# A norm row loaded once and spread over the partitions by products with ones, and the first chunk prepared ahead of the sample

## The chip, the core and the metric

The kernel runs on one core of a Trainium2 chip. A core has TensorE (matrix products, and turning of tiles by a product with the identity), VectorE, ScalarE and GpSimd (elementwise work), and SyncE, which mostly issues transfers. Transfers are issued from SP's and ACT's queues and run on 16 shared DMA engines. The metric is the time of one execution in microseconds, as the median of several runs.

## What is computed

One step of a decoder trunk of two layers: a retention layer with 4 heads, then a sliding-window attention layer. The prompt has 1024 tokens and the sample 8 tokens, all of 1024 features in f32. What matters here is the head of the first layer:

```python
def rmsnorm(x, g):
    xf = x.astype(jnp.float32)
    y = xf * lax.rsqrt(jnp.mean(xf * xf, axis=-1, keepdims=True) + EPS)
    return (y * g.astype(jnp.float32)).astype(x.dtype)

def retention_layer(x, S0, g_norm, w_in, g_out, w_out):
    h = rmsnorm(x, g_norm)
    proj = h @ w_in        # 1024 x 6144: q, k, v and gate
    ...
```

The norm's gain g_norm is one row of 1024 values (4 KB). Every token, prompt or sample, is multiplied by it.

## The kernel before

The whole kernel is one program with the order of each engine's instructions written out by hand. The prompt is cut into eight chunks of 128 tokens, X[0] to X[7], with tokens on the partitions and 1024 features along the row; X[8] holds the 8 sample tokens. Each chunk goes through the same steps, each a small helper:

- xload (L426): the transfer of the chunk, on SP's queue.
- sq (L431): ScalarE squares the chunk and sums each row.
- pw (L435 and L120): GpSimd turns the sum into one over the root, in two small instructions.
- sc (L440): VectorE multiplies the chunk by that column and by gb, the norm row spread over all 128 partitions.
- TR (through tr, L105): TensorE turns the chunk in eight 128 by 128 products into two banks of PSUM.
- hi and lo (L457, L461): ScalarE rounds the turned chunk to the short form, and VectorE takes the remainder; keep (L465) copies it back.

The first weights, a set called q0 with four tiles A11, A12, A21 and A22, are split in the same way by w_hi (ScalarE, L221) and w_lo (GpSimd or VectorE, L226). The first products are 16 "plain" groups of 24 products each (L544); chunks 1 and 3 to 7 are prepared between these groups, in an order given slot by slot. After them come the products of the projection by a seven-product scheme, the retention stage, and the second layer.

The program's start is written out in order: memsets, the load of gb as a broadcast of the 4 KB row to 128 partitions on ACT's queue (L866), the identity on the same queue (L867), the loads of chunk 0, the sample, chunk 2, two q0 tiles, chunks 1 and 3, two tiles of the next set, and chunks 4, 6 and 7 on SP's queue. Then the squares and roots of the sample, of chunk 0 and of chunk 2; the sample is scaled and turned first (eight small products into p8), then chunk 0 is scaled and turned. VectorE copies p8 to rdec and scales chunk 2, TensorE turns chunk 2, and hi, lo, w_hi and w_lo of chunks 0 and 2 and of A11 and A12 follow. Engines take their instructions in the written order, so an instruction that waits holds up those behind it on its engine.

The buffers called raw, five in turn, hold weight tiles and chunk 7. Chunks 4, 5 and 6 and the sample share three buffers called u; chunk 5 takes the sample's.

Of the kernel before, what the change touches and what calls it, by code (L numbers as in the profile page):

```python
# [7 lines left out]
F32 = mybir.dt.float32  # L8
# [6 lines left out]
D = 1024  # L15
# [45 lines left out]
def trunk(tc, x_prompt, x_sample, state_ret, cache_k, cache_v, norm_ret, w_in_ret, ret_out_norm,  # L61
          w_out_ret, norm_swa, w_in_swa, q_norm, k_norm, sinks, w_out_swa, c1, c2,
          y_p, y_s, nrp, nrs, nkp, nvp, nks, nvs):
    nc = tc.nc
    ctx = ExitStack()
    with ctx:
        ctx.enter_context(tc.manual_schedule(engines=MS))
        _trunk(ctx, tc, nc, locals())


def _trunk(ctx, tc, nc, a):
    x_prompt, x_sample, state_ret = a["x_prompt"], a["x_sample"], a["state_ret"]
    cache_k, cache_v = a["cache_k"], a["cache_v"]
    norm_ret, ret_out_norm, norm_swa = a["norm_ret"], a["ret_out_norm"], a["norm_swa"]
# [22 lines left out]
    mm = nc.tensor.matmul  # L97
# [6 lines left out]
    def tr(out, in_, ident, start=True, stop=True):  # L104
        nc.tensor.matmul(out, in_, ident, is_transpose=True, start=start, stop=stop)  # L105
# [13 lines left out]
    def rsq(out, in_, n):  # L119
        nc.gpsimd.tensor_tensor(out, in_, mhalf[:in_.shape[0], :n], ALU.pow)  # L120
# [13 lines left out]
    dcp = sa.enter_context(tc.tile_pool(name="dcp", bufs=1, reuse_waits="tile"))  # L134
    wq = sa.enter_context(tc.tile_pool(name="wq", bufs=1, reuse_waits="tile"))
# [26 lines left out]
    def bank(i, t):  # L162
        return abp.tile([128, 512], F32, tag=f"b{i}{t}", name=f"b{i}{t}")
# [7 lines left out]
    act, dve, pool = nc.scalar.activation, nc.vector, nc.gpsimd  # L171
# [238 lines left out]
    gb = sp.tile([128, D], F32, name="gb")  # L410
# [6 lines left out]
    def xload(c):  # L417
        if c in (0, 1, 2, 3):
            X[c] = xq.tile([128, D], F32, tag="xq", bufs=4, name="xq")
        elif c == 7:  # L420
            X[c] = raw_tile()
        else:
            X[c] = sp.tile([128, D], F32, tag="u", bufs=3, name="u")
        if c == 8:
            X[c] = X[c][0:ND, :]
        nc.sync.dma_start(out=X[c], in_=x_sample[:, 0, :] if c == 8 else x_prompt[0, c * 128:c * 128 + 128, :])  # L426

    def sq(c):
        SS[c] = sp.tile([128, 1], F32, name="ss", bufs=4)
        n = X[c].shape[0]  # L430
        act(junk[:n], X[c], AF.Square, accum_out=SS[c][:n])  # L431

    def pw(c):
        n = X[c].shape[0]
        pool.tensor_scalar(SS[c][:n], SS[c][:n], 1.0 / D, EPS, MUL, ADD)  # L435
        rsq(SS[c][:n], SS[c][:n], 1)

    def sc(c):
        n = X[c].shape[0]
        dve.scalar_tensor_tensor(X[c], X[c], SS[c][:n], gb[:n], MUL, MUL)  # L440

    def TR(c, b):

        PO[c] = [bank(b, j).rearrange("p (k t) -> p k t", k=4) for j in range(2)]
        for j in range(2):
            for k in range(4):
                tr(PO[c][j][:, k, :], X[c][:, 512 * j + k * 128:512 * j + k * 128 + 128], ident)
# [415 lines left out]
    for r in range(2):  # L863
        pool.memset(oneh[:, r, r:r + 1], 1.0)
    pool.memset(rdec32, 0.0)
    nc.scalar.dma_start(out=gb, in_=norm_ret[0].partition_broadcast(128))  # L866
    nc.scalar.dma_start(out=ident, in_=a["c1"][:, 0:128])  # L867
    act(warm, warm, AF.Silu)
    for c in (0, 8, 2):
        xload(c)  # L870
# [5 lines left out]
        raw_load(k0, r, nc.sync)  # L876
    for c in (4, 6, 7):
        xload(c)
    for c in (8, 0, 2):
        sq(c)  # L880
        pw(c)
    sc(8)
    p8 = vdp.tile([128, 8, ND], F32, tag="vd", name="pd8")
    for k in range(8):
        tr(p8[:, k, :], X[8][:, k * 128:k * 128 + 128], ident[:ND, :ND])
    sc(0)
    TR(0, 1)
    dve.tensor_copy(rdec, p8)
    sc(2)
    TR(2, 2)  # L890
# [1357 lines left out]
    out = so_all()  # L2248
# [159 lines left out]
```

## Time and profile before

| What | Value |
|---|---|
| median of 3 runs | 1294.03 us (1293.03 to 1294.62) |
| time of the profiled execution | 1293.47 us |
| its span, first to last instruction | 1291.7 us |
| TensorE busy | 1268.1 us, 98% |
| VectorE, GpSimd, ScalarE busy | 766.3, 741.4, 668.2 us |
| moved by the DMA engines | 206.69 MB |

The profile is of one execution; the time around the span, 1293.47 less 1291.7, belongs to the start and end of the program. Starts in the views are counted from the first instruction of the span.

### The profile page before, as it was taken

To read this page: it belongs to the slowest core of one execution; us is meant where nothing else is said; L and a number is where in the kernel's file an instruction comes from. 1 tells how busy PE (TensorE), PEld (TensorE's weight loads), DVE (VectorE), ACT (ScalarE), POOL (GpSimd) and SP (SyncE) were. 2 spreads that over 40 slices of the span, in tenths; PEclk is the share of its full clock that TensorE was granted. 3 is DMA by queue.
4 is the path that set the end of the run, shared out by engine and by line. 5 is a ranking of instruction groups with operands and counts; after the bars stand their busy time and mean duration, and the time that the engine had idled before them with its cause. 6 is when DMAs were issued, how large, how long until landed. Compare 5 with 4: busy or idle time off the path is not lost.

```text
span 1291.7 us, 26846 instructions
## 1 busy us (share of the span) xinstructions
PE 1268.1 (98%) x9839; PEld 1216.2 (94%) x9839; DVE 766.3 (59%) x1474; ACT 668.2 (52%) x1656; POOL 741.4 (57%) x886
## 2 busy tenths in 40 slices
PE   6999999999999999999999999999999999999998
PEld 5999999999999999988889999999999999998998
DVE  5954646665576764476763656855566666765321
ACT  5533445454555554588761234545575766765121
POOL 5654444535359899798771458636585767544000
PEclk9999999999999999999999999999998999999999
DMA  6313857677667673556879855833031221137232
GB/s 227 108 54 121 253 183 237 179 253 218 186 210 226 192 239 107 180 173 218 255 211 261 229 195 153 272 113 103 15 118 50 66 66 58 54 119 249 78 92 79
DMA packets 221967, 206.69 MB, mean 160 GB/s; under 512 B 32728, under 2 KB 196820, under 8 KB 221820
## 3 DMA queue, kind: packets, MB, share of 16 engines
q1 hardware_dynamic: 189840, 170.61, 43.8%
q10 hardware_dynamic: 31996, 34.36, 8.2%
q8 instruction: 78, 1.28, 0.4%
q14 instruction: 53, 0.43, 0.1%
HBM read 135.41 MB, written 70.55 MB: 159 GB/s over the span
## 4 chain that ended last, share of the span: by engine, by line
PE 90%; DVE 3%; DMA 2%; POOL 1%; ACT 1%; issue 1%; SPq 0%; ACTq 0%; DVEq 0%; POOLq 0%
PE b L335 8%; PE b L336 8%; PE b L337 8%; PE S L1302 7%; PE pj L1661 6%; PE pj L1662 6%; PE pj L1663 6%; PE b L328 4%; PE tr L105 4%; PE b L329 4%; PE b L330 4%; PE o L2023 2%; PE b L544 1%; PE sc L1986 1%; PE S L335 1%; PE S L336 1%
## 5 line engine op out<-in xcount | busy, mean ns | idle before, releaser
L335 PE MATMUL b<-xh,woh 128*128 128x258 f32 x784 | 223.2, 285 | 0.0
L337 PE MATMUL b<-xh,wol 128*128 128x258 f32 x784 | 221.7, 283 | 0.0
L336 PE MATMUL b<-xl,woh 128*128 128x258 f32 x784 | 221.6, 283 | 0.0
L1661 PE MATMUL pj<-SA,wh 128*128 128x384 f32 (+1 forms) x496 | 169.3, 341 | 1.5 <-ACT SA L2043 1.3
L1662 PE MATMUL pj<-SA,wh 128*128 128x384 f32 (+1 forms) x496 | 159.4, 321 | 0.2 <-DVE SA L2044 0.2
L1663 PE MATMUL pj<-SA,wl 128*128 128x384 f32 (+1 forms) x496 | 159.4, 321 | 0.0
L335 PEld LDWEIGHTS b<-xh,woh 128*128 128x128 f32 x784 | 148.0, 189 | 4.1 <-issue 3.7
L336 PEld LDWEIGHTS b<-xl,woh 128*128 128x128 f32 x784 | 148.7, 190 | 0.0
L337 PEld LDWEIGHTS b<-xh,wol 128*128 128x128 f32 x784 | 148.0, 189 | 0.0
L226 POOL TENSOR_TENSOR wol<-raw,woh 128x512 fp32r<-128x512 f32 x51 | 66.2, 1306 | 120.3 <-ACT woh L221 109.2
L328 PE MATMUL b<-woh,xh 128*128 128x256 f32 x448 | 126.6, 283 | 0.0
L329 PE MATMUL b<-wol,xh 128*128 128x256 f32 x448 | 126.0, 281 | 0.0
L330 PE MATMUL b<-woh,xl 128*128 128x256 f32 x448 | 125.6, 280 | 0.0
L1661 PEld LDWEIGHTS pj<-SA,wh 128*128 128x128 f32 x496 | 94.1, 190 | 5.1 <-issue 2.4
L1662 PEld LDWEIGHTS pj<-SA,wh 128*128 128x128 f32 x496 | 94.3, 190 | 0.4 <-DVE SA L2044 0.4
L2001 POOL TENSOR_TENSOR s<-s,sm 128x512 f32<-128x512 f32 x64 | 66.6, 1041 | 48.2 <-DVE sm L2000 43.2
L1663 PEld LDWEIGHTS pj<-SA,wl 128*128 128x128 f32 x496 | 93.9, 189 | 0.0
L328 PEld LDWEIGHTS b<-woh,xh 128*128 128x128 f32 x448 | 84.3, 188 | 5.0 <-issue 2.9
L330 PEld LDWEIGHTS b<-woh,xl 128*128 128x128 f32 x448 | 84.3, 188 | 0.0
L329 PEld LDWEIGHTS b<-wol,xh 128*128 128x128 f32 x448 | 84.3, 188 | 0.0
L1993 ACT ACTIVATE s<-s,mx 128x257 f32<-128x257 f32 x128 | 64.2, 505 | 34.9 <-DVE mx L1991 34.2
L221 ACT ACTIVATE woh<-s 128x512 fp32r<-128x512 f32 x88 | 54.1, 624 | 54.4 <-POOL s L211 20.7
(530 smaller groups left out, 3622.6 us busy)
## 6 DMA issues: line engine op xcount, KB each, us to landing
raw<-in_w_in_ret_dram ACTq DMA_DIRECT2D x44, 512.0 KB
st<-in_state_ret_dram SPq DMA_DIRECT2D x64, 256.0 KB
out_dram<-st SPq DMA_DIRECT2D x64, 256.0 KB
vb<-vscr SPq DMA_DIRECT2D x64, 128.0 KB
evp<-qks SPq DMA_DIRECT2D x32, 256.0 KB
evx<-vsc SPq DMA_DIRECT2D x32, 256.0 KB
wr<-in_w_in_swa_dram SPq DMA_DIRECT2D x32, 256.0 KB
evc<-gsc SPq DMA_DIRECT2D x16, 256.0 KB
```

Of the source, the lines that this page charges most:

```text
L226: eng.tensor_tensor(lo, src_of(s, name, sub), hi.bitcast(F32), SUB)
L328: mm(dst, xh, wh, start=a and i == 0, stop=False, skip_group_check=True)
L329: mm(dst, xh, wl, start=False, stop=False, skip_group_check=True)
L330: mm(dst, xl, wh, start=False, stop=z, skip_group_check=True)
L335: mm(dst, wh, xh, start=a, stop=False, **sg)
L336: mm(dst, wh, xl, start=False, stop=False, **sg)
L337: mm(dst, wl, xh, start=False, stop=z, **sg)
L1302: mm(box[0], s.op[f"A{i + 1}{j + 1}", 0][w][:, k, :], xs_[t][x[j]][:, k, :], start=(xs_ is XH and w == 0 and j + k == 0), stop=(xs_ is XL ...
L1661: mm(ps, hi[:, k, fs], xh[:, k, t0:t1], start=first and k == ks[0], stop=False)
L1662: mm(ps, hi[:, k, fs], xl[:, k, t0:t1], start=False, stop=False)
L1663: mm(ps, lo[:, k, fs], xh[:, k, t0:t1], start=False, stop=last and k == ks[-1])
L2001: nc.gpsimd.tensor_tensor(st[:, :, 0:256], st[:, :, 0:256], sm.unsqueeze(2).broadcast_to([128, 2, 256]), ALU.mult)
```

## The change

The norm row is loaded as it is, 4 KB, into the first partition of a raw buffer. A row of 128 ones (row1) is made by VectorE. Two products of the ones with the halves of the row put the row on all partitions of two PSUM banks, and VectorE copies these to gb. The order of the first three chunks becomes chunk 0, sample, chunk 2 for the squares and roots; chunk 0 is scaled and turned ahead of the sample's scaling and turning.

```diff
-    nc.scalar.dma_start(out=gb, in_=norm_ret[0].partition_broadcast(128))
+    grow = wq.tile([1, D], F32, tag="raw", bufs=5, name="raw")
+    nc.scalar.dma_start(out=grow, in_=norm_ret[0:1, :])
     nc.scalar.dma_start(out=ident, in_=a["c1"][:, 0:128])
+    row1 = dcp.tile([1, 128], F32, name="row1")
+    dve.memset(row1, 1.0)
     act(warm, warm, AF.Silu)
...
-    for c in (8, 0, 2):
+    bank_of = {}
+    for j in range(2):
+        bank_of[0, j] = bank(0, j)
+        mm(bank_of[0, j], row1, grow[:, 512 * j:512 * j + 512], start=True, stop=True)
+    for j in range(2):
+        dve.tensor_copy(gb[:, 512 * j:512 * j + 512], bank_of[0, j])
+    for c in (0, 8, 2):
         sq(c)
         pw(c)
+    sc(0)
+    TR(0, 1)
     sc(8)
     p8 = vdp.tile([128, 8, ND], F32, tag="vd", name="pd8")
     for k in range(8):
         tr(p8[:, k, :], X[8][:, k * 128:k * 128 + 128], ident[:ND, :ND])
-    sc(0)
-    TR(0, 1)
     dve.tensor_copy(rdec, p8)
     sc(2)
     TR(2, 2)
```

## Rows read from the trace of the kernel before

**Rows 1.** The page, busy time of TensorE, its share of the span, instructions.

```profile
PE 1268.1 (98%) x9839; PEld 1216.2 (94%) x9839; DVE 766.3 (59%) x1474; ACT 668.2 (52%) x1656; POOL 741.4 (57%) x886
```

**Rows 2.** Stretches: length, TensorE's busy time and instructions, granted clock, DMA share, GB/s.

```profile
24.00:53.20 29.20, 28.78 (x242) 1.00 0.23 71
53.20:500.00 446.80, 446.80 (x3762) 1.00 0.64 194
```

**Rows 3.** Chain of waits of the start: start, length, what.

```profile
1.17 5.33 DMA u<-in_x_sample_dram
...
8.94 1.01 POOL ss L435
...
10.02 0.58 POOL ss L120
...
11.97 1.97 PE b L105 x8
...
16.91 3.81 POOL wol L226 x3
...
50.83 1.21 DVE raw L440
```

**Rows 4.** Queues (packets, MB) to 2.5, 3.0, 6.5 us; 6.5 to 7.0; SP's wait.

```profile
q1 hardware_dynamic: 21, 0.09, 21.4%
...
q10 hardware_dynamic: 16, 0.07, 5.3%
...
q1 hardware_dynamic: 215, 0.78, 39.2%
q10 hardware_dynamic: 288, 0.59, 29.6%
...
6.50:7.00 0.50, 0.00 (x0) 0.00 (x0) 0.00 (x0) 0.48 (x1) 0.00 (x0) 1.00 1.00 410
...
SPq L426 <- DMA gb<-in_norm_ret_dram: 2.5, 1, 2.5
```

**Rows 5.** Timeline to 38 us: start, length, engine, line, what, idle time before.

```profile
0.72 0.41 ACTq L866 DMA_DIRECT2D gb<-in_norm_ret_dram  x1
...
7.70 1.06 ACT L431 ACTIVATE junk<-xq 128x1024 f32<-128x1024 f32 x1
...
9.94 1.02 PE L105 MATMUL pd<-ident,u 8*128 8x8 f32 x8 [9.94 <-DVE u L440]
...
11.83 0.22 DVE L888 COPY rdec<-pd 128x64 f32<-128x64 f32 x1
...
12.64 1.28 DVE L440 SCALAR_TENSOR_TENSOR xq<-xq,ss,gb 128x1024 f32<-128x1024 f32 x1 [0.59 <-POOL ss L120]
...
15.78 0.74 PE L544 MATMUL b<-xh,woh 128*128 128x258 f32 x4
...
19.82 1.12 PE L544 MATMUL b<-xh,woh 128*128 128x258 f32 x8
...
21.65 2.30 DVE L440 SCALAR_TENSOR_TENSOR xq<-xq,ss,gb 128x1024 f32<-128x1024 f32 x1 [3.41 <-POOL ss L120]
...
21.75 1.13 PE L544 MATMUL b<-xl,woh 128*128 128x258 f32 x8
...
24.10 1.06 PE L105 MATMUL b<-ident,xq 128*128 128x128 f32 x8 [1.23 <-DVE xq L440]
...
36.78 1.15 ACT L481 ACTIVATE xh<-xq 128x512 fp32r<-128x512 f32 x2 [1.53 <-DMA gl<-in_norm_swa_dram]
```

**Rows 6.** Lines: an f32 product of 512 columns; copies of a PSUM bank; ns min/median/max.

```profile
L344 PE MATMUL vd<-raw,rdec x64: 592/592/617, 76.8 to 331.6; 128*32 128x512 f32 x64
...
L465 DVE COPY xq<-b x4: 673/678/679, 17.0 to 25.1; 128x512 f32<-128x512 f32 x4
```

**Rows 7.** Line L105, turning products before 15.2 us and after 24, ns min/median/max.

```profile
L105 PE MATMUL b<-ident,xq x14: 364/421/477, 12.0 to 15.1; 128*128 128x128 f32 x14
...
L105 PE MATMUL b<-ident,xq x16: 271/273/302, 24.1 to 28.7; 128*128 128x128 f32 x16
```

## The prediction

> **What bounds the kernel now.** I read the page first: TensorE is busy for 98% of the span [rows 1]. So only two things can move the time: less TensorE work, or TensorE starting sooner. The change does not remove TensorE work, so I went to the stretches [rows 2]. From 53.2 to 500 us TensorE is busy for all of 446.8 us; from 24 to 53.2 it lacks 0.4 us; before 24 lie its waits. The change sits wholly at the start, before the plain products at 15.78 [rows 5]. A gain there is worth what it takes off the moment when TensorE begins its unbroken work, and no more; after it everything is issued relative to what came before, so the shift should be carried to the end.
>
> Next the chain of waits for the start [rows 3]. It begins with the load of the sample's chunk (landed at 6.50), then ScalarE's sums of squares, GpSimd's root for chunk 0 (its first half takes 1.01 us), VectorE's scaling of chunk 0, TensorE's turning of chunks 0 and 2, and the conversion of the second weight tile, after which GpSimd starts three weight remainders at 16.91. From there the chain runs through GpSimd and VectorE to the scaling of chunk 7 at 50.83, and joins TensorE there. TensorE and this second chain arrive together: TensorE waited 1.23 us for chunk 1 at 24.10 and then all but 0.4 us of the way was work. Hence the quantity to forecast is the shift of GpSimd's start at 16.91.
>
> **The transfers.** The broadcast row is 512 KB and goes on ACT's queue beside chunk 0 (512 KB) on SP's. Up to 6.5 us the two queues had moved 0.59 and 0.78 MB [rows 4]: the row took about half of what moved. It falls to 4 KB. When does chunk 0 land then? Up to 2.5 us SP's queue had moved 0.09 MB, all chunk 0 at that time. Left are 0.524 - 0.09 = 0.43 MB and 0.066 MB of the identity; at the 410 GB/s of [rows 4] that is 1.2 us: 3.7 us is the lower bound. The same sum for the kernel before (1.15 MB up to the sample, less 0.09) gives 5.1, and the sample landed at 6.5, 1.4 later; so 5.1 is the upper bound. I take 4.3, nearer the lower, since less than half the bytes can lag. SP also waited 2.5 us at chunk 3's load for the broadcast to land [rows 4]; that goes, but ScalarE squares chunk 3 only behind the first plain group [rows 5], so it is worth nothing.
>
> The 4 KB row itself: a 4 KB load later in the kernel kept ScalarE waiting 1.53 us [rows 5], so it took at least about that; the sample's load took 5.33 [rows 3]. Issued at 0.72 as the broadcast was [rows 5], it lands between 2.2 and 6.1. ACT's queue moves its first packets between 2.5 and 3.0 [rows 4], and this row is the first on it: I take 3.2.
>
> **The products and copies.** No row shows a product with one partition. The nearest is the f32 product of 512 columns, 592 ns [rows 6], taken late at the faster rate. Early on the same turning products take 421 ns against 273 later [rows 7], and eight of them 1.97 us [rows 3] against 1.06 [rows 5]. The granted-clock column reads 1.00 throughout [rows 2]; the durations say otherwise, and I read the early ones as the 1.2 GHz level. So a product costs between 0.59 and 1.18 us; I take 1.18, since TensorE has done nothing before. Two products end at 3.3 + 2.4 = 5.7, and the second copy out of the bank (0.68 [rows 6]) makes the row ready at 6.4; the first copy hides under the second product. Copies and products lie where TensorE was idle until 9.94 and VectorE until it scaled the sample just before that [rows 5]. The memset of the ones, the extra buffer turn (chunk 7 now takes the row's buffer, and its load is the last of those on SP) and SP's own order cost nothing for the same reason. Bounds for the ready time: 2.2 + 1.2 + 0.7 + 0.2 = 4.3, and 6.1 + 2.4 + 0.7 + 0.1 = 9.3.
>
> **The new order.** Chunk 0 at 4.3: squares 1.06 and the reading of the sum, 1.15 together (squares 7.70 to 8.76 [rows 5], the sum read just behind); GpSimd's two small steps with nothing beside them about 0.95 more (their first half has 1.01 in the chain because of company, their second 0.58 [rows 3]; I take the first at under 0.4). So its scaling can start at 6.4, just when the row is ready. That first half took 1.01 before because VectorE's scaling of the sample ran beside it; now it is free, and the sample's own step pays instead.
>
> From the scaling's start S, step by step: 1.28 + 0.06, turning of chunk 0 1.97, then the sample's eight small turns 1.02 (its scaling, from about S + 1.9 to S + 3.2, is done by then), then the copy of them on VectorE 0.22 with gaps, together S + 4.65, and only then chunk 2's scaling, which stands behind that copy on VectorE. Before, chunk 2's scaling waited for GpSimd's root alone (12.64 [rows 5]); that root now ends near S + 3.8. So the reordering puts a new wait in front of chunk 2: 0.65 us is given back there, since sample landing to chunk 2 was 12.64 - 6.50 = 6.1 and is now 2.1 + 4.65 = 6.75.
>
> With S = 6.4, chunk 2 is scaled at 11.05 instead of 12.64: 1.6 us sooner, and with it its turning, the weight conversion and GpSimd's 16.91. ScalarE reaches chunk 2's squares at about 6.7, after the load. The sample moves later by a little; its columns and the reload of its buffer (chunk 5, squared among the plain groups) have slack.
>
> **Sum.** Span 1291.7 - 1.6 = 1290.1; 1.8 us lie outside the span (1293.47 - 1291.7), so 1291.9; the profiled execution stood 0.56 under the median of 1294.03. Forecast 1292.4. Bounds: S = 5.8 (early chunk, fast products) gives -2.2; chunk 0 at 5.1 gives S = 7.2 and -0.8; a row ready only at 9.3 gives +1.3.
>
> **The clock.** Before, the turns run without a gap from 11.97, and the first plain products at 15.78 run at the fast rate (four in 0.74 us, the pace of the later blocks of eight in 1.12 [rows 5]). After, TensorE's work comes as islands: products until 5.7, turns 7.8 to 10.8, a gap of 1.6, turns from 12.4. The faster level may come later. A group of 24 plain products takes 2.9 us at the fast rate (three blocks, 19.82 to 21.75 and 1.0 more [rows 5]), so it would lose up to 2.9 at half of it. Up to 24.10 TensorE has 1.2 us of waiting to absorb this. The Trainium skill (TensorE: Matmul & The Clock Gate, Part 4) says that transposes don't count as busy for the clock; by it the islands would change nothing, the plain products would start slow in both kernels, the sum would stay and the third rival would have no chance. The trace disagrees: the plain products at 15.78 ran at the fast pace with only turns before them [rows 5].
>
> **Rivals.** (1) *The row or chunk 0 comes late.* If the row lands after 4.75, S + 4.65 passes 12.64 and the start is later than before; at the bound it is +1.3, so 1295.3. If chunk 0 doesn't land sooner at all (6.4), the change does not do what it is for: S = 8.5, +0.5, 1294.5. For it: nothing shows a lone 4 KB row in a loaded start. Against: it is first on its queue, and half the bytes ahead of chunk 0 are gone. With gains under 0.8: 0.18. (2) *More is gained.* Chunk 1's scaling took 2.30 us instead of 1.28 beside a weight remainder on GpSimd [rows 5]; if it slips past that one, another 1.0 comes off exactly where TensorE waits: -2.6, 1291.4; with S at its low bound -3.2, 1290.8. Chance 0.17. (3) *The clock, and slower.* If the 1.2 GHz level holds past the second plain group, two groups cost 5.8, less the 1.2 of waiting and the 1.6 gained: +3.0, 1297.0. It decides from the end of the first group: one alone costs 2.9 against those 2.8, no change. Against: turns alone raised the rate before. Chance 0.05.
>
> **How the numbers follow.** The forecast with its own range of 1291.6 to 1293.2 gets 0.58, and 0.02 stays for what I don't see. About 0.2%, 2.6 us, is what can be told from no change here; the three runs spread over 1.6. Faster by more than that needs 1291.4 or less: rival 2 and the forecast's lower tail, 0.18. Slower by that: rival 3 and little else, 0.05. The rest, 0.77, is within. The range of 1290.6 to 1294.4 leaves out the far ends of rivals 2 and 1 and all of 3.
>
> **What would show it.** Chunk 0 is squared first, at 4.3 (3.7 to 5.1); the row's two copies end by 6.4; chunk 0's scaling waits for one of the two; the sample's GpSimd step is now the long one; chunk 2's scaling starts straight after the small copy, near 11.05; GpSimd's three remainders start near 15.3 instead of 16.91; chunk 1's turning starts near 22.5; TensorE's work from 53.2 on keeps its length. It would be wrong if the three remainders start early and the end of chunk 7's turning doesn't follow, or if the clock's level after 12 us differs.

## The result, and the profile after

The changed kernel took 1296.79 us (median of 11, 1293.93 to 1299.29) beside 1293.32 for the kernel before on the same chip (11 runs): 1.0028 times as long, with a 95% interval of 1.0018 to 1.0038. That is 3.5 us slower where 1.6 us less was forecast, and outside the range. The profiled execution took 1298.41 us with a span of 1296.5, against 1293.47 and 1291.7: 4.8 us more span.

The page's line of TensorE, beside [rows 1]: 7.2 us more busy, with four more instruction records. Up to 24 us it is 5.4 more (16.70 against 11.26), of which the two products with ones are 3.7; the rest is mostly work at the slower rate.

```profile
PE 1275.3 (98%) x9843; PEld 1220.6 (94%) x9843; DVE 768.7 (59%) x1477; ACT 667.3 (51%) x1656; POOL 740.4 (57%) x886
```

The timeline of the start, in the columns of [rows 5]:

```profile
2.27 3.74 PE L885 MATMUL b<-raw,row 1*128 1x512 f32 x4 [2.27 <-DMA raw<-in_norm_ret_dram]
...
4.35 0.69 DVE L887 COPY gb<-b 128x512 f32<-128x512 f32 x1 [3.29 <-PE b L885]
...
4.75 1.06 ACT L431 ACTIVATE junk<-xq 128x1024 f32<-128x1024 f32 x1 [1.55 <-DMA xq<-in_x_prompt_dram]
...
6.05 0.69 DVE L887 COPY gb<-b 128x512 f32<-128x512 f32 x1 [1.01 <-PE b L885]
...
6.95 1.28 DVE L440 SCALAR_TENSOR_TENSOR xq<-xq,ss,gb 128x1024 f32<-128x1024 f32 x1 [0.21 <-POOL ss L120]
...
8.29 1.97 PE L105 MATMUL b<-ident,xq 128*128 128x128 f32 x8 [2.28 <-DVE xq L440]
...
10.30 1.02 PE L105 MATMUL pd<-ident,u 8*128 8x8 f32 x8
...
11.36 0.23 DVE L897 COPY rdec<-pd 128x64 f32<-128x64 f32 x1 [1.11 <-PE pd L105]
11.49 1.26 POOL L226 TENSOR_TENSOR wol<-raw,woh 128x512 fp32r<-128x512 f32 x1 [0.82 <-ACT woh L221]
11.50 2.33 DVE L440 SCALAR_TENSOR_TENSOR xq<-xq,ss,gb 128x1024 f32<-128x1024 f32 x1
...
13.89 1.97 PE L105 MATMUL b<-ident,xq 128*128 128x128 f32 x8 [2.56 <-DVE xq L440]
...
15.69 2.60 PE L544 MATMUL b<-xh,woh 128*128 128x258 f32 x8
...
17.08 3.76 POOL L226 TENSOR_TENSOR wol<-raw,woh 128x512 fp32r<-128x512 f32 x3 [4.33 <-ACT woh L221]
...
18.09 1.92 PE L544 MATMUL b<-xh,wol 128*128 128x258 f32 x8
...
19.81 1.30 PE L544 MATMUL b<-xl,woh 128*128 128x258 f32 x8
...
21.78 1.28 DVE L440 SCALAR_TENSOR_TENSOR xq<-xq,ss,gb 128x1024 f32<-128x1024 f32 x1 [3.37 <-POOL ss L120]
...
23.83 1.04 PE L105 MATMUL b<-ident,xq 128*128 128x128 f32 x8
```

The moved chain is there and is sooner: chunk 0 is scaled at 6.95, before the sample. But chunk 2's scaling takes 2.33 us instead of 1.28, because a weight remainder on GpSimd began 0.01 us before it, and the three remainders start at 17.08, where [rows 3] has 16.91. The plain products at 15.69 and 18.09 run at the slow pace (2.60 and 1.92 us for eight); the pace of 1.12 us for eight comes back only behind 19.81, where it was there at 15.78 before [rows 5]. Chunk 1's scaling escapes its collision (1.28 us instead of the 2.30 of [rows 5]), and chunk 1's turning starts at 23.83 against 24.10, without TensorE's wait of 1.23. At 32 us the changed kernel is 0.2 us behind. So in this execution the start gave nothing, in either direction.

The loss lies later. At 397 us TensorE waits 0.4 us for a weight remainder, and behind it the changed kernel is 0.9 us behind. The large step is at 546, in the retention stage: there the shift grows by about 4.4 us, to 5.2, and most of it stays (4.8 at the end). The waits of 536 to 552 us in the changed kernel (who, for whom: us in total, times, longest), first of the compute engines, then of SP's queue:

```profile
PE tr L105 <- DVE on L1076: 3.1, 1, 3.1
...
ACT Sh L1046 <- PE po L1031: 1.9, 1, 1.9
DVE sT L796 <- DMA gsc<-raw: 1.8, 1, 1.8
```

```profile
SPq L1561 <- DMA gsc<-raw: 1.8, 1, 1.8
```

And TensorE in two stretches (columns as in [rows 2]):

```profile
540.00:545.80 5.80, 2.94 (x16) 1.00 0.73 223
545.80:549.30 3.50, 3.26 (x13) 0.51 0.86 277
```

The timeline of the same place, kernel before and then kernel after:

```profile
540.24 0.28 DVE L796 TENSOR_TENSOR sT<-tr,M 128x128 f32<-128x128 f32 x1
...
542.29 0.66 PE L105 MATMUL tr<-ident,on 128*128 128x128 f32 x4 [0.22 <-DVE on L1067]
...
542.74 1.09 ACT L1037 ACTIVATE Sh<-S 128x512 fp32r<-128x512 f32 x2 [1.06 <-DMA gsc<-raw]
...
546.97 0.60 PE L105 MATMUL tr<-ident,on 128*128 128x128 f32 x4
```

```profile
545.04 0.29 DVE L796 TENSOR_TENSOR sT<-tr,M 128x128 f32<-128x128 f32 x1 [1.80 <-DMA gsc<-raw]
...
545.25 0.74 DVE L1076 TENSOR_SCALAR on<-po,ss 128x512 f32<-128x512 f32 x1
...
546.04 1.12 PE L105 MATMUL tr<-ident,on 128*128 128x128 f32 x4 [3.10 <-DVE on L1076]
...
552.22 0.60 PE L105 MATMUL tr<-ident,on 128*128 128x128 f32 x4
```

`sT` and `on` are made by VectorE; TensorE turns `on` with the identity. Before, TensorE waited 0.22 us for that; now `sT` waits for a transfer of a gate output (`gsc<-raw`), `on` stands behind it, and TensorE waits 3.10 us. Directly after this wait the granted clock is 0.51 for 3.5 us, the 1.2 GHz level, and the four turns take 1.12 us instead of 0.66. The wait, 2.9 us longer than before, and the slow work behind it together make the step of about 4.4: the next `on` is turned at 552.22 instead of 546.97.

### The profile page after: what moved, and what is told of

It reads as the page before. It is cut to its first block, busy times and chain, and to the rows that moved or that the text cites. A ratio compares the mean times of both kernels' runs of the same rounds, so it can differ in the third digit from the quotient of the medians.

```text
span 1296.5 us, 26857 instructions
## 1 busy us (share of the span) xinstructions
PE 1275.3 (98%) x9843; PEld 1220.6 (94%) x9843; DVE 768.7 (59%) x1477; ACT 667.3 (51%) x1656; POOL 740.4 (57%) x886
## 3 DMA queue, kind: packets, MB, share of 16 engines
q8 instruction: 78, 1.28, 0.4%
## 4 chain that ended last, share of the span: by engine, by line
PE 92%; DVE 3%; POOL 2%; ACT 2%; DMA 1%; issue 1%; ACTq 0%; SPq 0%; DVEq 0%; POOLq 0%
PE S L1311 9%; PE b L335 7%; PE b L337 7%; PE b L336 7%; PE pj L1670 6%; PE pj L1671 6%; PE pj L1672 6%; PE tr L105 4%; PE b L328 4%; PE b L329 4%; PE b L330 4%; PE o L2032 2%; PE b L544 2%; PE sc L1995 1%; PE S L335 1%; PE S L336 1%
```

## Why should the start touch 546 us? The theories

The raw buffers are a ring of five, and the 4 KB row takes one turn of it (`grow = wq.tile(..., tag="raw", bufs=5)`). So every later tenant of the ring sits one buffer further on. The last gate set's four outputs (p, x, c, w in `evac`) go into raw buffers and are stored from there; p is written last. The retention stage then lays its own tiles over the same memory. **Theory A**: the turn lays `sT0` over a late output, and `sT` has to wait until that output has been stored. **Rival B**: the loss comes from the start (later clock, other transfer times) or from any rotation, and what lies under `sT0` does not matter.

After e11 theory A had to be extended, to **A2**: the tile of ones (`row1`, 512 bytes on every partition) moves the rings by 512 bytes, and this lays `Sh0` over a tile that a product into `po` still reads. By the addresses of the compiled programs that tile is `vl`, the remainder of the values: it is the operand that moves through the second product into `po`, and in the kernel before it ends exactly where `Sh0` begins. The expectations of e12 and e13 call it "weights". **Rival C** of e12 to e14 was that these 1.8 us come from the ring's turn in some other way, or from the later start of the stage.

The letters change between the sets: in e1 to e3 theory C is the 512 bytes, and in e6 theory D is the 512 bytes or the row's load into a raw buffer.

Each kernel was run 11 or 12 times, in turn with the kernel before (29 to 35 runs on the same chip); ratios have 95% intervals. None of these kernels leaves out any part of the computation.

## The experiments

**e1: the row outside the ring, no tile for the ones** (on the changed kernel).

```diff
-    grow = wq.tile([1, D], F32, tag="raw", bufs=5, name="raw")
+    grow = gb[0:1, :]
-    row1 = dcp.tile([1, 128], F32, name="row1")
+    row1 = M01[0:1, 0:128]
```

> The changed kernel, but the norm row is loaded into the first partition of gb itself and the ones lie in a table's buffer that is filled much later: no raw buffer and no new memory is taken. Theory A (the row takes one turn of the five raw buffers, so that the last gate outputs, written out late, lie under the retention stage's first tiles): TensorE's wait for chunk on at 546 us goes from 3.1 back to under 0.7 us, the low clock behind it goes, and the time comes to 0.999 to 1.001 of before. Theory B (the loss is at the start: chunk 2's scaling of 2.33 us beside a weight remainder and the clock that rises at 20 us): the wait may go, but the time stays at 1.002 to 1.004. Theory C (the 512 bytes of the ones shift the layout): as A here. The row may be ready 0.5 us later, since the copies write what the products read.

Measured: 1293.61, ratio 0.9999 [0.9989, 1.0010]. The loss is gone, and with it the wait and the low clock (the granted clock is 1.00 all through 536 to 553 us). Theory B had the time stay at 1.002 to 1.004:

```profile
541.26 0.66 PE L105 MATMUL tr<-ident,on 128*128 128x128 f32 x4 [0.18 <-DVE on L1076]
...
542.55 1.09 ACT L1046 ACTIVATE Sh<-S 128x512 fp32r<-128x512 f32 x2 [1.47 <-DMA gsc<-raw]
```

**e2: the turn alone** (on the kernel before).

```diff
+    dve.memset(raw_tile()[0:1, 0:1], 0.0)
     nc.scalar.dma_start(out=gb, in_=norm_ret[0].partition_broadcast(128))
```

> The kernel before with one raw buffer taken and left unused at the start, nothing else. Theory A: TensorE waits about 3 us at 546 us, the granted clock falls behind it, and the time is 1.002 to 1.004 of before, with an unchanged start. Theories B and C: no difference, 0.999 to 1.001.

Measured: 1.0014 [1.0003, 1.0024], with the start as before. One turn of the ring and one tiny memset make the kernel slower. It is a miss in size: the expected time was 1.002 to 1.004 behind a wait of about 3 us, the wait is 2.4, and no low clock follows it in this profile. The waits show where:

```profile
DVE sT L796 <- DMA gsc<-raw: 3.1, 1, 3.1
...
PE tr L105 <- DVE on L1068: 2.4, 1, 2.4
```

**e3: only the ones moved out of their tile**; the row stays in the ring (second half of e1's diff).

> The changed kernel with only the ones moved to the later table's buffer, so that no tile's address shifts by 512 bytes; the row still takes a raw buffer. Theory A: nothing changes, 1.002 to 1.004 of before and a wait of about 3 us at 546. Theory C: the wait goes and the time is 0.999 to 1.001. Theory B: 1.002 to 1.004 too, but told from A by the first kernel of this set.

Measured: 1.0023 [1.0012, 1.0033]. Wait and low clock stay, so the 512 bytes are not needed for them; that they do nothing does not follow, as e6 showed. Beside e1 this is the clearest test of the turn: the two kernels differ in the row's buffer alone, and their intervals don't meet (1.0023 [1.0012, 1.0033] against 0.9999 [0.9989, 1.0010]). The waits, and TensorE's stretch:

```profile
DVE sT L796 <- DMA gsc<-raw: 4.1, 1, 4.1
...
PE tr L105 <- DVE on L1076: 3.4, 1, 3.4
```

```profile
545.80:549.30 3.50, 3.50 (x12) 0.52 0.92 292
```

**e4: e1, and chunk 2's scaling ahead of the small copy.**

```diff
-    dve.tensor_copy(rdec, p8)
     sc(2)
+    dve.tensor_copy(rdec, p8)
     TR(2, 2)
```

> The first kernel of this set, and the copy of the sample's turned columns stands behind chunk 2's scaling on VectorE instead of ahead of it. All theories: chunk 2 is scaled at about 10.7 us for 1.28 us instead of at 11.5 for 2.33, its turning starts near 12.1 instead of 13.9, and GpSimd's three remainders start near 15.3. Theory B: with both losses of the start gone the time falls 1.5 to 3.5 us under the first kernel's. Theory A: 1.0 to 1.6 us under the first kernel's, 0.998 to 0.9995 of before.

Measured: 1291.43, ratio 0.9979 [0.9970, 0.9988]. It is faster than both kernels. It lies 2.2 us under e1, more than theory A gave (1.0 to 1.6) and within theory B's 1.5 to 3.5; since times resolve about 1.3 us, this does not decide, and e1's own time had spoken against B. Chunk 2's scaling now runs before GpSimd's first remainder, at its own 1.28 us, and chunk 1 is turned without a wait at 22.02, against 24.10:

```profile
10.91 1.28 DVE L440 SCALAR_TENSOR_TENSOR xq<-xq,ss,gb 128x1024 f32<-128x1024 f32 x1 [0.46 <-POOL ss L120]
...
12.27 0.23 DVE L898 COPY rdec<-pd 128x64 f32<-128x64 f32 x1
...
15.45 3.78 POOL L226 TENSOR_TENSOR wol<-raw,woh 128x512 fp32r<-128x512 f32 x3 [1.66 <-ACT woh L221]
...
22.02 1.03 PE L105 MATMUL b<-ident,xq 128*128 128x128 f32 x8
```

**e5: the row alone**, outside the ring and in the order of before (the load, products and copies of the change with e1's two tiles).

> The kernel before with the 4 KB row and the two products alone (row in the first partition of gb, ones in the later table's buffer), sample still first. Theory A (all of the loss came from the raw turn; the transfer by itself brings chunks sooner): the sample lands near 4.7 instead of 6.5, its scaling waits for the row at about 7 instead of 8.6, GpSimd's remainders start 1.0 to 1.6 us sooner and the time is 0.9985 to 0.9995 of before. Theory B (products on a slow TensorE and the clock eat the gain): 0.9995 to 1.001.

Measured: 0.9984 [0.9973, 0.9995], at the edge of what theory A gave. Chunk 1's turning starts at 22.94, 1.16 us sooner than before.

**e6: five turns**: the changed kernel with four more turns (the added line, four times), so that the ring stands as before.

```diff
     grow = wq.tile([1, D], F32, tag="raw", bufs=5, name="raw")
+    dve.memset(raw_tile()[0:1, 0:1], 0.0)
```

> The changed kernel with four more raw buffers taken and left unused behind the row's, five turns in all: the row still takes a raw buffer and the 512 bytes stay, but the last gate outputs fall into the same buffers of the ring as before. Theory A: the wait at 546 us goes (under 0.7), no low clock there, 0.999 to 1.001 of before. Theory D (it is the load of the row into a raw buffer itself, or the shift by 512 bytes): still about 3 us of wait and 1.002 to 1.004.

Measured: 1.0004 [0.9995, 1.0013]. A miss in part: `sT` no longer waits for a transfer and there is no low clock at 546, but TensorE still waits 1.8 us, and `Sh` waits for `po`:

```profile
ACT Sh L1050 <- PE po L1035: 1.9, 1, 1.9
PE tr L105 <- DVE on L1080: 1.8, 1, 1.8
```

**e7: three turns** (on the kernel before, e2's line three times).

> The kernel before with three raw buffers taken and left unused at the start. Theory A in its sharper form: what counts is which of the last four gate outputs lies under which first tile. Here the second of them to be written out lies under the first score tile (sT), and the last under the first state tile (Sh): the score tile waits under 1 us, ScalarE's state step waits 2 to 3 us instead of 1.1, TensorE's wait at 546 us is 0.3 to 2, and the time is 1.000 to 1.002. In its blunt form (any rotation costs the same): 3 us at 546 and 1.002 to 1.004.

Measured: 0.9996 [0.9985, 1.0006]; TensorE's wait is 0.2, and ScalarE's `Sh` waits 1.9 us for a transfer. All three lie just under what was expected (1.000 to 1.002, 0.3 to 2 us, 2 to 3 us). Not every rotation costs: here w lies under `sT0`, and `sT` does not wait for it.

**e8: the broadcast kept**, 512 KB on SP's queue behind chunk 0 and the sample; no products; chunk 0 first and e4's order.

> No products: the broadcast of 512 KB as before, but on SP's queue behind chunk 0 and the sample, with the order of e4 (chunk 0 first, copy behind chunk 2's scaling). Theory A: chunk 0 lands near 4.5, the row near 6.3, chunk 0 is scaled near 6.6 instead of 7 to 8, TensorE starts its turns 0.4 to 1.3 us sooner than in e4, and the time is 0.997 to 0.9985 of before. If the broadcast lands after 7.5 or holds up chunk 2's load, the time is that of e4 or above it, 0.998 to 0.9995.

Measured: 0.9984 [0.9974, 0.9995]. Chunk 0 is squared at 4.66 and chunk 1 turned at 22.00. So the gain does not need the 4 KB row: a full broadcast out of the way of chunk 0 does as well, and spares products and copies.

**e9: another layout**: the changed kernel as it stands, with `sT0` and `sTh0` moved away from under p.

```diff
-    lay("Sh1", "Sl1", "sT0", "sTh0", "sTl0", "qh0", "ql0", "kh0", ...
+    lay("Sh1", "Sl1", "ql0", "sT0", "sTh0", "sTl0", "qh0", "kh0", ...
```

> The changed kernel as it stands (row in the ring of raw buffers), with one line of the retention stage's layout reordered: ql0 now lies where sT0 and sTh0 lay, over the raw buffer of the gate output that is written last, and sT0, sTh0, sTl0 and qh0 lie 1 KB further on. Theory A (sT0 has to wait until the transfer out of that buffer has landed, and the turning of on behind it): sT no longer waits for a transfer, TensorE's wait for on at about 546 us falls from 3.1 to under 0.7, no stretch at the lower clock stands there, and the time is that of the kernel with the row outside the ring, 0.9985 to 1.0010 of before. Rival B (the turn costs by moving transfers or loads, and what lies under sT0 does not matter): the wait stays at 2.4 to 3.4 and the time at 1.0015 to 1.0035. If ql0 has to wait instead, GpSimd shows a wait for the transfer at ql, and some of the loss stays.

Measured: 1.0017 [1.0004, 1.0030]. The time is a miss for theory A alone and lies in rival B's range, but the wait, 1.8 us, is below B's 2.4 to 3.4. The trace shows why: the transfer's wait at `sT` and the low clock are gone, and the same 1.8 us as in e6 is left, again with `Sh` waiting for `po`:

```profile
ACT Sh L1046 <- PE po L1031: 1.9, 1, 1.9
PE tr L105 <- DVE on L1076: 1.8, 1, 1.8
```

**e10: e9 with e4's order.**

> As the kernel with the other layout, and chunk 2's scaling issued ahead of the small copy of the turned sample. By theory A the two repairs add up: no wait above 0.7 us at about 546, chunk 1's turning at about 22 us instead of 24.1, and the time 0.9970 to 0.9990 of before, like the kernel that keeps the row outside the ring and has the same order (0.9979). By rival B the wait stays and the time is 1.0000 to 1.0015.

Measured: 1.0002 [0.9992, 1.0013]: a miss for A alone and the time that B gave. The wait is 1.8 us, with no transfer waited for at `sT`. Chunk 1's turning starts at 22.73, where about 22 was expected.

**e11: the layout alone**, on the kernel before.

> The kernel before with the reordered layout alone: the control. In it the gate output that is written last lies in another raw buffer, so the order of these tiles should not matter: by theory A TensorE's wait for on at about 542 stays under 0.7 and the time is 0.9990 to 1.0010 of before. If the layout is worth something by itself, for a reason outside theory A, the time is below 0.9985, and the gain of the other two is not A's.

Measured: 1.0004 [0.9992, 1.0015], TensorE's wait for `on` 0.2. The layout by itself is worth nothing that the time shows.

The kernels with 1.8 us left (after, e6, e9, e10) have the tile of ones in common. That gave A2 and three more runs.

**e12: both overlays taken away**: e9 with e3's line; the row is still in the ring.

> The changed kernel with its row in the ring, the other order of the retention stage's tiles (ql0 where sT0 and sTh0 lay) and the ones in a mask's place instead of a tile of their own, so that no ring moves by 512 bytes. Theory A2 (two overlays: the ring's turn lays sT0 over the last-written gate output; the 512 bytes of the ones lay Sh0 over the weights of a product into po, so Sh waits for po and on comes late): with both gone TensorE's wait for on at about 542 is under 0.7 us, Sh at about 538.5 is released by S and not by po, and the time is 0.9985 to 1.0010 of before. Rival C (the 1.8 us left in the other-layout runs comes from the ring's turn in some other way, or from the later start of the stage): the wait stays near 1.8 and the time is 1.0005 to 1.0025.

Measured: 1.0004 [0.9994, 1.0014]. It differs from e3 by the layout's line alone, and e3 stood at 1.0023. As A2 said, the wait for `on` is 0.2 and `Sh` is released by `S`. But a third wait stands later: SP's load of the masks (`M23`) waits 2.4 us for a gate output to be stored, and TensorE waits 2.0 us, up to 549.01, for a load that stands behind it on SP's queue. That the one makes the other late is read from the order on that queue; no run takes `M23`'s overlay away by itself. The waits:

```profile
PE tr L779 <- DMA evp<-qks: 2.0, 1, 2.0
...
PE tr L105 <- DVE on L1076: 0.2, 1, 0.2
```

```profile
SPq L1561 <- DMA gsc<-raw: 2.4, 1, 2.4
```

**e13: the 512 bytes alone** (on the kernel before).

```diff
+    row1 = dcp.tile([1, 128], F32, name="row1")
+    dve.memset(row1, 1.0)
```

> The kernel before with nothing but the one-partition tile of ones (512 bytes on every partition) and its memset. Theory A2: Sh0 lies over the weights of the product into po; Sh waits 1.9 us for po, TensorE waits 1.6 to 2.0 us for on at about 544, and the time is 1.0005 to 1.0020 of before, with the start as before. Rival C: nothing moves, the wait stays at 0.2 and the time is 0.9990 to 1.0010.

Measured: the trace is as A2 said, to the tenth of a microsecond:

```profile
ACT Sh L1039 <- PE po L1024: 1.9, 1, 1.9
PE tr L105 <- DVE on L1069: 1.8, 1, 1.8
```

The time is 1.0003 [0.9994, 1.0012], under the expected 1.0005 to 1.0020, whose lower half the interval holds. So the 512 bytes are shown by the wait, and by the time only in part: in executions with the same mean granted clock e13 is 1.0 to 1.7 us the slower (at 0.996, for instance, a median of 1295.59 over 6 runs beside 1293.88 over 17). Not all of that need be theirs, since its profile also has a wait of 0.6 us at 461.

**e14: e12 with e4's order.**

> The kernel with both overlays repaired, and chunk 2's scaling issued ahead of the small copy. Theory A2: no wait above 0.7 us at about 542, chunk 1's turning 1.0 to 2.1 us sooner than before, and the time 0.9970 to 0.9990 of before, like the kernel with the row outside the ring and the same order (0.9979). Rival C: the wait of 1.8 stays and the time is 0.9995 to 1.0010, like the kernel with only the layout reordered and this order (1.0002).

Measured: 0.9995 [0.9985, 1.0006]: a miss for A2 on the time, which is the one that rival C gave, without C's wait. The waits for `on` are gone, SP's wait for `M23` stays at 1.7 and TensorE's at the late load at 1.2: part of e4's gain is eaten there.

**The three overlays side by side.** What lies under which tile is read from the addresses of the compiled programs; the waits are those of each profile in us.

```
kernel   rings   under sT0  sT waits   under Sh0     Sh waits  under M23  SP waits  TensorE's wait
         +512 B             for store                for po               for store for on
before   no      -          no         -             no        c          no        0.2
e13      yes     -          no         vl            1.9       c          no        1.8
e6       yes     -          no         vl            1.9       c          no        1.8
e2       no      p          3.1        -             no        -          no        2.4
e3       no      p          4.1        -             no        x          1.5       3.4
after    yes     p          1.8        vl            1.9       x          1.8       3.1
e9       yes     -          no         vl            1.9       x          1.7       1.8
e12      no      -          no         -             no        x          2.4       0.2 (2.0 later)
e1, e4   no      -          no         -             no        c          no        0.2
```

e10 stands as e9 (SP waits 1.6) and e14 as e12 (SP 1.7, TensorE 1.2 later). e5, e8 and e11 have none of the three; e7 has w under `sT0` and no wait there.

Each wait stands in exactly those kernels in which its overlay stands. Together they do not add up: in the changed kernel `Sh`'s lateness covers a part of `sT`'s wait (1.8 instead of e3's 4.1; VectorE had waited 3.0 us for `Sh` just before).

## Why the prediction was wrong, point by point

**The step that failed** is in "The products and copies": the memset of the ones and "the extra buffer turn ... cost nothing", since they lie where the engines were idle. That is true of their own time and misses where their memory lies. The turn puts `sT0` under p's store and `M23` under x's; the ones' 512 bytes put `Sh0` over a tile, `vl`, that is still read. e2 shows the turn's part by itself (1.0014), e13 the ones' wait (1.8 us), and e1 takes all of it away (0.9999). No rival had this mechanism; the nearest, rival 3, named the clock at the start, and the low level came at 546, behind the wait.

In the two profiles the sum reads: forecast 1.6 us less; measured 0.2 more at the start, 0.6 more at 397, 4.4 more at 546, and about 0.4 given back later, in all 4.8 more span.

**The start** was right in kind and too large in size. Right: the row's products early, chunk 0's scaling first and waiting, chunk 2's scaling straight behind the small copy (11.36, then 11.50), S + 4.55 after the scaling's start where S + 4.65 was forecast (e4 takes that wait away and gains). Its terms:

- The row landed at 2.27 (forecast 3.2; 3.3 in e4 and e5).
- The two products took 3.74 us, not 2.4: each left two records of about 1.05 us. The copies of 0.69 were as forecast (0.68). The row was ready at 6.74, not 6.4.
- Chunk 0 was squared at 4.75, not 4.3, and scaled at 6.95, not 6.4.
- Chunk 2's scaling began at 11.50, not 11.05, and then met GpSimd's remainder. The prediction knew this collision for chunk 1 [rows 5] and had no term for it at chunk 2. It is decided by 0.1 us: in e1 VectorE began at 11.37 and GpSimd at 11.47, and then it was the remainder that took 2.31:

```profile
11.37 1.28 DVE L440 SCALAR_TENSOR_TENSOR xq<-xq,ss,gb 128x1024 f32<-128x1024 f32 x1
11.47 2.31 POOL L226 TENSOR_TENSOR wol<-raw,woh 128x512 fp32r<-128x512 f32 x1 [1.08 <-ACT woh L221]
...
12.70 1.97 PE L105 MATMUL b<-ident,xq 128*128 128x128 f32 x8 [1.51 <-DVE xq L440]
...
23.08 1.07 PE L105 MATMUL b<-ident,xq 128*128 128x128 f32 x8 [1.23 <-DVE xq L440]
```

The forecast chose the shift of GpSimd's three remainders as the measure of the start. By it the start gave -0.2 us after (17.08), 1.0 in e1 (15.90) and in e12 (15.91), and with the copy moved behind 1.5 in e4 (15.45), against the forecast of 1.6. Chunk 1's turning, the other sign, shows more than that (0.3 after, 1.0 in e1, 1.4 in e12, 2.1 in e4).

**Rival 2**, chunk 1's scaling past its collision, did occur in the profile after (1.28 us at 21.78), but TensorE was then busy with products at the slow pace until 23.83, so nothing was gained by it. **Rival 3's** mechanism is seen in this profile: the fast pace came some 4 us later than in the one before, and TensorE's former wait of 1.23 at 24.10 absorbed the loss, as the prediction said of one group. That the change is the cause is not shown: e7, e11 and e13, whose start is that of the kernel before, also began their plain products at the slow pace (2.51 to 2.60 us for eight at 15.7), and in e1, e3 and e9, with the new start, the fast pace was there by 18.0.

**Carried to the end**: the reading was right as far as the chain goes. The remainders' shift is carried almost unchanged to the scaling of chunk 7: e4 1.46 and then 1.39 us sooner, e5 1.15 and 1.14, e1 1.01 and 1.00, after 0.17 and 0.22 later. The scaling before, after and in e4:

```profile
50.74 1.28 DVE L440 SCALAR_TENSOR_TENSOR raw<-raw,ss,gb 128x1024 f32<-128x1024 f32 x1
```

```profile
50.96 1.28 DVE L440 SCALAR_TENSOR_TENSOR raw<-raw,ss,gb 128x1024 f32<-128x1024 f32 x1
```

```profile
49.35 1.27 DVE L440 SCALAR_TENSOR_TENSOR raw<-raw,ss,gb 128x1024 f32<-128x1024 f32 x1
```

The times of e4 and e5 (2.7 and 2.1 us less than before) agree with these shifts within what times resolve.

**What stays open.** The 0.4 us at 397 came in some kernels and not in others (after 0.4, e14 0.3, e3 0.2), and a step of the same kind, TensorE waiting for a weight remainder whose weights came late to ScalarE, stands at 461 us in e2, e7, e10 and e13 (0.4 to 0.7). e9, whose memory is laid out as e10's, has none, so an overlay of this kind is not the reason; the cause is not settled. Times resolve about 0.1%, or 1.3 us: e6 and e9 have the same wait of 1.8 us and medians of 1.0004 and 1.0017; of that difference only SP's wait for `M23` (in e9 alone) is seen. That the low clock comes from the wait before it is argued, not shown: it stood behind waits of 3.1 and 3.4 us (after, e3), and not behind 2.4 (e2), 2.0 (e12) or 1.8 (e6, e9, e10, e13); and between 969 and 976 us TensorE waits 2.9 to 3.0 us for `sq` in all sixteen profiles, each time with a low clock behind it. In the profile of e11 TensorE waits 1.6 us for `Sl`, which no other profile has and the theories do not explain. A version with the row in the ring and all three overlays removed was not made; e1 and e4 are that version without the ring.

## What to carry to other kernels

An extra tile in a ring of buffers, or a small new tile below it, is not free because its instruction is hidden: it moves every later tenant of that memory, and a stage that lays its tiles over the ring may then wait for a store or a reader that had been done in time. Ask of each new tile what lies over it at the end of the ring's life, or place it in memory that is there anyway (here a row of `gb` and a corner of a mask). And when a new order puts a two-input VectorE instruction close to one on GpSimd, price it for both outcomes.

## What the runs showed of the hardware

- VectorE's scaling of a chunk and a weight remainder on GpSimd did not share in the rows read: the one that began first kept its own time (1.26 to 1.30 us), the other took 2.29 to 2.33 although it had begun only 0.01 to 0.14 us later. The Trainium skill (SBUF — State Buffer, "SBUF: two separate sides") says that the port pair of the two engines is locked by whoever starts first, and that the other blocks for the whole instruction. The rows of after and e1 agree, with the roles exchanged between them.
- A product of one partition by 512 f32 columns left two records of 1.05 us each at the start, and two such products took 3.74 us together; the row of [rows 6] has 0.59 for one record late in the kernel.
- A load of 4 KB issued at 0.72 landed at 2.3 in some profiles and at 3.3 to 3.4 in others (after, e1, e3, e9 and e12 against e4, e5, e6, e10 and e14).
- In the profile after, the turns of chunks 0 and 2 (1.97 us each) stand apart, with small turns and 2.56 us of idle time between, and the plain products behind them ran at the slow pace (2.60 us for eight). In e5 sixteen turns ran for 3.98 us on end, and the plain products at 14.36 took 0.88 us for four. The rule cited in the prediction, that transposes do not count for the clock (the Trainium skill, TensorE: Matmul & The Clock Gate, Part 4), would have the plain products start slow in both; e5 disagrees, like the kernel before and e2 (0.91 us for four). But e7, e11 and e13 also had sixteen turns on end, and there the plain products were slow (1.23 us for four, where the kernel before has 0.74), as by the rule. So the islands are not shown to be the cause of the slow pace.
- The granted clock differs between executions late in the program too. Behind the wait for `sq` (2.93 us up to 971.17 before, 2.90 up to 969.86 in e4) it is 0.66 over 970 to 980 us in the profile before, and 0.83 in that of e4. The mean goes with the time: of the 35 runs of the kernel before beside e1, the ten at 0.999 have a median of 1291.85 us and the seventeen at 0.996 one of 1294.82. What decides between them is not known.
